# Hybrid decoder trunk: the first head pair's forget-gate projection ahead of its recurrence-gate products

## The chip, the cores and the metric

One Trainium2 chip, and one of its eight cores. The metric is the device time of one execution in microseconds (us); less is better. Five engines run side by side, each through its own instruction list in order: PE (matrix products), ACT (activations and copies), DVE (elementwise work on vectors), POOL (a second, slower elementwise engine), and SP, which here only issues transfers. They wait for each other through semaphores.

## The reference, cut to what matters

One layer on 1024 positions of width 1024: a norm, two token mixers side by side, a projection, then an MLP. The change touches the two mixers of one head pair:

```
proj = h @ w_in
xa, ga, q, f, v, g, m_a, m_b = jnp.split(proj, SPLIT_POINTS, axis=-1)
xa = causal_depthwise_conv(xa, conv_w, conv_b)
# first mixer: recurrence with two gates, one 256x256 block for each pair of heads
r = sigmoid(xb @ w_r + b_r);  i = sigmoid(xb @ w_i + b_i)
a = exp(-8 * r * softplus(-lam));  u = sqrt(-expm1(2 * log_a)) * (i * xf);  h = scan(a, u)
# second mixer: linear attention with a forget gate
f_gate = lb + (1 - lb) * sigmoid(f);  kf = (1 - lb) * sigmoid(-f);  qf = silu(q)
o = hgrn2_chunkwise(qf, kf, log(f_gate), v)
```

## The kernel before, in words

The mixers run in eight stages: two halves of the sequence (512 positions each, `c`) times four head pairs (256 channels, `p`); `stage(i)` with `i = 4c + p` issues the projections of one pair. A projection (`project_steps`) of a pair makes two PSUM banks of 128x512 from 16 pairs of 128x128 weights and 128x512 activations. Each product is done as three (high x high, high x low, low x high), for accuracy, so a projection is 48 products in eight pieces of six; between pieces the generator yields. The weights come in 128x1024 tiles: one transfer by SP, a cast on ACT (L94, the high part `wH`), and a subtraction on DVE (L98, the low part `wL`). Three such pairs of tiles fit at a time, so a cast waits for the products that read the tiles three earlier.

Stage 0 issues, in the order of the code: xa, the convolution of xa (`conv`, DVE L586, L98 for its split into `xcH` and `xcL`), q, five of the eight pieces of f, the products of the recurrence's gates (`rg_lru`: 24 products from `xcH`, `xcL` into `pr`, `pi` for each half `s` of the pair, four sigmoids, exp and tanh at L612, then DVE L633 to L644), the other three pieces of f, and `f_of` (two sigmoids of each bank at L671 and L672, which make `f` and `kk`, and DVE L673 and L674). Stage 0 runs alone.

Then `hgrn(i)` runs for each pair. It is mainly a chain on DVE (L681: products of decays with q and with k, into `qa`, `qb`, `kb`, `kc`, `kk`, `qf`), with a few blocks of small products on PE: three of scores (L691), then L811 and L822, transposes (L848), state updates (L858), outputs (L883, L886). `go(n)` issues n pieces of the next stage's projections ahead of such a block, so that PE has work while the chain goes on; for the first pair the numbers are GO_FIRST = (16, 5, 2, 1, 2), 16 pieces (xa and q of pair 1) to the third block and 5 more to L811. PE's order is held as the code has it, from the end of xa of stage 0 on. The orders of ACT and DVE are set by a scheduler when the program is built, from its own estimate of when each operand is ready, with the weight splits (`split_w`) at a higher priority.

PSUM banks come in rings by tag: `pj` has four (a projection takes two, and `pr`, `pi` of half 0 take two), `sc` two (`pr`, `pi` of half 1, and score blocks) and `hg` two.

Of the kernel before, what the change touches and what calls it, by code (L numbers as in the profile page):

```python
# [45 lines left out]
def trunk(ctx: ExitStack, tc: tile.TileContext, x, wts, mlp, pv, gains, mask_f, mask_u, out):  # L46
# [148 lines left out]
    def transposed(xn, dst, tt, name):  # L195
        for h in range(2):
            pt = bank("hg", f"xT_{name}_{h}")
            for k in range(4):
                pin(PE.transpose(pt[:, k * P : (k + 1) * P], xn[:, (4 * h + k) * P : (4 * h + k + 1) * P], ident))
            cut = slice(tt * P, (tt + 1) * P)  # L200
            split(pt.rearrange("p (k t) -> p k t", k=4), dst[0][h][:, :, cut], dst[1][h][:, :, cut])
# [59 lines left out]
    def parameters():  # L261

        tc.keep_in_program_order(V.tensor_tensor(out=t3, in0=lbl, in1=lbl, op=ALU.max))
        V.tensor_tensor(out=t3, in0=lbl, in1=t3, op=ALU.subtract)
        A.activation(t4, t3, AF.Sigmoid, scale=-1.0)
        A.activation(t3, t3, AF.Sigmoid)
        V.reciprocal(t4, t4)
        V.tensor_tensor(out=t3, in0=t3, in1=t4, op=ALU.mult)
        V.reciprocal(t4, t3)
        V.tensor_tensor(out=t3, in0=t3, in1=t4, op=ALU.mult)  # L270
        V.tensor_tensor(out=lb, in0=t3, in1=t3, op=ALU.subtract)
        V.tensor_scalar(lb, lb, 0.0, 1.0, op0=ALU.max, op1=ALU.min)
        V.tensor_scalar(omlb, lb, -1.0, 1.0, op0=ALU.mult, op1=ALU.add)

        V.tensor_scalar(t3, lam, -1.0, None, op0=ALU.mult)
        V.tensor_tensor(out=t4, in0=t3, in1=lam, op=ALU.min)
        A.activation(t4, t4, AF.Sigmoid)
        V.tensor_scalar(t5, t4, -1.0, 2.0, op0=ALU.mult, op1=ALU.add)
        V.reciprocal(t5, t5)
        V.tensor_tensor(out=t4, in0=t4, in1=t5, op=ALU.mult)  # L280
        V.tensor_tensor(out=t5, in0=t4, in1=t4, op=ALU.mult)
        V.tensor_scalar(t6, t5, 1.0 / 17, 1.0 / 15, op0=ALU.mult, op1=ALU.add)
        for n in (13, 11, 9, 7, 5, 3, 1):
            V.tensor_tensor(out=t6, in0=t6, in1=t5, op=ALU.mult)
            V.tensor_scalar(t6, t6, 1.0 / n, None, op0=ALU.add)
        V.tensor_tensor(out=t6, in0=t6, in1=t4, op=ALU.mult)
        V.tensor_scalar(t3, t3, 0.0, None, op0=ALU.max)
        V.scalar_tensor_tensor(t3, t6, 2.0, t3, op0=ALU.mult, op1=ALU.add)
        V.tensor_scalar(sp4, t3, 4.0, None, op0=ALU.mult)
        V.tensor_scalar(nsp8, t3, -8.0, None, op0=ALU.mult)  # L290
# [180 lines left out]
    def next_rows(tt, behind, square_behind=None):  # L471
        xt = tile_x(f"x{4 + tt}")
        nc.sync.dma_start(xt, x[(4 + tt) * P : (5 + tt) * P, :])
        xn = xt_pool.tile([P, D], F32, tag="xn", name=f"xn1{tt}", bufs=2)
        norm_rows(xt, xn, gain0[0], f"x1{tt}", behind, square_behind)
        return xn
# [30 lines left out]
    def combos_on(n):  # L507
        for _ in range(n):
            next(piece_parts.pop(0))

    def project_steps(c, name):

        pp = [bank("pj", f"pj_{name}_{s}") for s in range(2)]
        for half in range(2):
            wh, wl = next_w()
            for k in range(4):
                hh, hl = kt(hT[c], 4 * half + k)
                for s in range(2):
                    cols = slice(k * 256 + s * P, k * 256 + (s + 1) * P)
                    mm3(pp[s], wh[:, cols], wl[:, cols], hh, hl, half == 0 and k == 0, half == 1 and k == 3)  # L520
                if half == 0 or k < 3:
                    yield
        return pp
# [39 lines left out]
    def conv_in(c, p, pp):  # L563
        xc = mt("xc", f"xc{c}{p}", (P, 2, T))
        xps = []
        for s in range(2):
            u = 2 * p + s
            xp = mt("xp", f"xp{c}{u}", (P, T + 16), bufs=2)
            A.copy(xp[:, 3 : T + 3], pp[s])
            A.activation(  # L570
                xc[:, s, :],
                pp[s],
                AF.Identity,
                bias=pvt[:, PV_CB + u : PV_CB + u + 1],
                scale=pvt[:, PV_CW + 24 + u : PV_CW + 25 + u],
            )
            xps.append(xp)
        return xc, xps

    def conv(c, p, xc, xps, behind=None):  # L580
        for s in range(2):
            u = 2 * p + s
            xp = xps[s]
            V.tensor_copy(xp[:, 0:3], xcar[:, u, :])
            for j in range(3):
                ins = V.scalar_tensor_tensor(  # L586
                    xc[:, s, :],
                    xp[:, j : j + T],
                    pvt[:, PV_CW + 8 * j + u : PV_CW + 8 * j + u + 1],
                    xc[:, s, :],  # L590
                    op0=ALU.mult,
                    op1=ALU.add,
                )
                if behind is not None:
                    how = mybir.DependencyInfo(mybir.DependencyClass.NoSync, mybir.DependencyReason.DATA)
                    tc.add_manual_dep(ins.ins, behind.ins.name, how, reason="behind")
            if c + 1 < NC:
                G.tensor_copy(xcar[:, u, :], xp[:, T : T + 3])
        xh = mt("xcH", f"xcH{c}{p}", (P, 2, T), F32R)
        xl = mt("xcL", f"xcL{c}{p}", (P, 2, T), F32R)  # L600
        split(xc, xh, xl)
        return xc, xh, xl
# [311 lines left out]
    def hooked(steps, hooks):  # L914
        n = 0
        while True:
            try:
                next(steps)
            except StopIteration as end:
                return end.value  # L920
            n += 1
            if n in hooks:
                hooks[n]()
            yield

    def v_of(i):
        def between(tt):
            if tt == 0:
                gots[i - 1]["tail"]()
            if tt == (2 if i == 2 else 1):  # L930
                on_T(*where(i - 2), gots[i - 2])
            for n in {}.get((i, tt), ()):
                with tc.high_priority(400):
                    transposed(xn1[n], hT[1], n, f"x1{n}")

        yield from v_steps(*where(i - 1), gots[i - 1], between)

    def stage(i):
        c, p = where(i)
        got = gots[i]  # L940
        if i > 1:
            yield from v_of(i)

        def more(n):
            with tc.high_priority(400):
                transposed(xn1[n], hT[1], n, f"x1{n}")

        hooks = {at: lambda n=n: more(n) for at, n in {2: ((4, 1),), 3: ((2, 2), (6, 3))}.get(i, ())}
        px = yield from hooked(project_steps(c, f"xa{c}{p}"), hooks)
        xc, xps = conv_in(c, p, px)  # L950
        if i == 0:
            parameters()
            tc.keep_in_program_order(V.tensor_copy(mu, mu32.to_broadcast([P, 7, 8, 32])))
            pinned[0] = True
        yield
        if i == 1:
            gots[0]["tail"]()
            transposed(xn1[0], hT[1], 0, "x10")
        if i > 4:
            combos_on(2)  # L960

        def convolve():
            got["xc"] = conv(c, p, xc, xps, None)

        pq = yield from hooked(project_steps(c, f"q{c}{p}"), {} if i == 1 else {6: convolve})
        got["q1"] = q_of(c, p, pq)
        yield
        fs = hooked(project_steps(c, f"f{c}{p}"), {6: convolve} if i == 1 else {})
        for _ in range(5 if i != 1 else 7):
            next(fs)  # L970
            yield
        if i > 3:
            combos_on(1 if i == 4 else 2)
        if i == 1:
            pf = yield from fs
            got["f"], got["kk"] = f_of(c, p, pf)
            yield
        yield from rg_lru(c, p, got, *got["xc"])
        if i > 0:
            gots[i - 1]["normalised"]()  # L980
        for n in ((0,), (1,), (2, 3))[i] if i < 3 else ():
            if i == 0:
                xn1[n] = next_rows(n, behind_first[1], behind_first[0])
            else:
                xn1[n] = next_rows(n, gots[0]["states"] if i == 1 else None)
        if i != 1:
            pf = yield from fs
            got["f"], got["kk"] = f_of(c, p, pf)

# [770 lines left out]
    for kb in range(n_kb):  # L1760
        last = kb + 1 == n_kb
        qs = order[2 * kb : 2 * kb + 2]
        for half in range(2):
# [33 lines left out]
            for step, (bk, wo, uo), prs in [  # L1797
# [14 lines left out]
                for pr in prs:  # L1812
                    _, ci, cj, op = ADDS[step]
# [95 lines left out]
```

## Time and profile before

| what | value |
|---|---|
| time, median of 3 runs | 1535.8 us (1534.24 to 1536.2) |
| the profiled execution's own time | 1535.65 us |
| its span on the profile | 1533.9 us |
| granted clock of PE in it | 0.999 |
| busy in the span: PE, DVE, ACT, POOL | 99%, 75%, 53%, 10% |

The profile is of one execution. A page gives busy times, the chain of work that ended last and the costliest groups; a trace behind it lists every instruction with its start and, in brackets, how long its engine had stood still before it and what ended that. Names are those of the program without numbers, so `pj_f` is either bank of the projection f, of whichever stage runs then. Stage 0 takes the first 64 us or so, pair 0's `hgrn` goes on to about 113 us. Starts of consecutive products lie closer than their lengths, since PE overlaps them.

### The profile page before, as it was taken

What the parts mean: (1) busy time and instruction counts of PE and PEld (TensorE: products, weight loads), DVE (VectorE), ACT (ScalarE), POOL (GpSimd) and SP (SyncE); (2) the same over time, 40 slices, a digit from 0 to 9 for tenths busy, and PEclk for the clock granted to TensorE, in tenths of its full rate; (3) what the DMA queues carried; (4) which work ended last, traced back from release to release, by engine and by line L of the source; (5) the groups of instructions that cost most, each with busy time, mean ns of one, the idle gap of its engine ahead of it and who ended that gap; (6) DMA issues with size and microseconds to landing.
All of it is one profiled execution on the core that took longest, in us unless ns stands there. A gap on an engine that the chain in (4) does not pass through costs nothing. (4 is left out here: it accounts for less than half of the span.)

```text
span 1533.9 us, 23245 instructions
## 1 busy us (share of the span) xinstructions
PE 1521.5 (99%) x9091; PEld 1275.1 (83%) x9091; DVE 1148.0 (75%) x1661; ACT 806.4 (53%) x1346; POOL 152.3 (10%) x191
## 2 busy tenths in 40 slices
PE   9999999999999999999999999999999999999998
PEld 7878988889889888888888888888888888888886
DVE  6798696485675828786856568888788998888777
ACT  6646757567567435454533447766666722111115
POOL 1021210232614600000000000000000000000000
PEclk9999999999999999999999999999999999999999
DMA  8545455465664284432328323666666766666642
GB/s 300 198 154 200 143 193 198 150 217 173 226 230 143 97 299 160 159 137 83 138 97 327 138 110 145 267 247 247 247 252 249 262 259 264 252 248 249 240 194 110
DMA packets 82255, 306.82 MB, mean 200 GB/s; under 512 B 8545, under 2 KB 21985, under 8 KB 69218
## 3 DMA queue, kind: packets, MB, share of 16 engines
q1 hardware_dynamic: 78832, 295.24, 52.2%
q10 hardware_dynamic: 3314, 10.10, 1.7%
q8 instruction: 71, 1.16, 0.3%
q14 instruction: 38, 0.31, 0.1%
HBM read 201.50 MB, written 103.81 MB: 199 GB/s over the span
## 5 line engine op out<-in xcount | busy, mean ns | idle before, releaser
L1795 DVE TENSOR_TENSOR acc<-acc,dX 128x512 f32<-128x512 f32 x128 | 85.1, 685 | 27.7 <-PE dX L157 27.0
L94 ACT CAST wA<-q 128x512 fp32r<-128x512 f32 x46 | 28.6, 622 | 119.3 <-PE dX L157 95.4
L98 DVE TENSOR_TENSOR wL<-raw,wH 128x1024 fp32r<-128x1024 f32 x46 | 56.2, 1224 | 41.1 <-ACT wH L94 40.9
L157 PE MATMUL po<-wH,y 128*128 128x512 f32 x256 | 80.6, 391 | 0.0
L94 ACT CAST wH<-raw 128x1024 fp32r<-128x1024 f32 x46 | 48.2, 1049 | 34.2 <-DMA raw<-wts_in 14.2
L1695 POOL TENSOR_TENSOR gx<-acc,gain 128x256 f32<-128x256 f32 x1 | 0.7, 743 | 605.4 <-DVE acc L1795 605.4
L157 PEld LDWEIGHTS po<-wH,y 128*128 128x128 f32 x256 | 48.1, 188 | 9.8
L1795 DVE TENSOR_TENSOR acc<-acc,dY 128x512 f32<-128x512 f32 x64 | 43.6, 687 | 14.2 <-PE dY L157 13.8
L157 PE MATMUL po<-wL,y 128*128 128x512 f32 x128 | 49.8, 389 | 0.0
L1543 ACT ACTIVATE b<-b 128x512 f32<-128x512 f32 x48 | 30.0, 626 | 28.3 <-DVE b L1542 28.1
L98 DVE TENSOR_TENSOR wA<-q,wA 128x512 fp32r<-128x512 f32 x46 | 31.5, 686 | 15.1 <-ACT wA L94 15.1
L157 PE MATMUL uX<-h2B11H,wA 128*128 128x512 f32 x128 | 42.1, 390 | 0.0
L120 ACT CAST wH<-raw 128x1024 fp32r<-128x1024 f32 x36 | 37.8, 1049 | 8.2 <-issue 3.7
L192 POOL TENSOR_TENSOR rstd_h<-rstd_h,mhalf 128x1 f32<-128x1 f32 x8 | 4.6, 585 | 371.2 <-DVE rstd_h L187 371.2
L586 DVE SCALAR_TENSOR_TENSOR xc<-xp,pvt,xc 128x512 f32<-128x512 f32 x48 | 40.0, 844 | 1.1 <-ACT xc L570 1.1
L157 PE MATMUL gX<-hT00H,wA 128*128 128x512 f32 x112 | 36.9, 390 | 0.0
L1102 DVE TENSOR_TENSOR s<-q,q 128x512 f32<-128x512 f32 x46 | 31.6, 687 | 5.1 <-DMA q<-mlp_in 4.8
L499 POOL TENSOR_TENSOR stt<-r,stt 128x256 fp32r<-128x256 f32 x16 | 19.8, 1261 | 126.3 <-ACT stt L498 114.2
L1110 DVE TENSOR_TENSOR s<-q 128x512 f32<-128x512 f32 x46 | 31.6, 686 | 0.2
L1544 ACT ACTIVATE b<-b 128x512 f32<-128x512 f32 x48 | 30.3, 631 | 1.0
L890 ACT ACTIVATE on<-po 128x128 f32<-128x128 f32 x64 | 16.9, 278 | 26.1 <-PE po L886 26.0
L157 PEld LDWEIGHTS uX<-h2B11H,wA 128*128 128x128 f32 x128 | 24.0, 188 | 5.0
(2327 smaller groups left out, 5298.8 us busy)
## 6 DMA issues: line engine op xcount, KB each, us to landing
q<-mlp_in SPq DMA_DIRECT2D x92, 512.0 KB, 3.8
raw<-wts_in SPq DMA_DIRECT2D x80, 512.0 KB, 4.7
rest<-wL SPq DMA_DIRECT2D x36, 512.0 KB, 2.9
wL<-rest SPq DMA_DIRECT2D x36, 512.0 KB, 4.0
hd<-ri SPq DMA_DIRECT2D x16, 256.0 KB, 3.7
od<-onT ACTq DMA_DIRECT2D x8, 512.0 KB, 6.5
cdT<-stT SPq DMA_DIRECT2D x16, 256.0 KB, 3.4
o<-od SPq DMA_DIRECT2D x4, 1024.0 KB, 7.8
```

The lines of the kernel that those rows point to most:

```text
L94: ins = casts[name] = A.copy(h, src)
L98: ins = V.tensor_tensor(out=lo, in0=src, in1=h.bitcast(F32), op=ALU.subtract)
L120: A.copy(h, raw)
L157: ins = PE.matmul(o, a, b, start=begins, stop=ends, **how)
L499: G.tensor_tensor(out=lo, in0=src, in1=h.bitcast(F32), op=ALU.subtract)
L586: ins = V.scalar_tensor_tensor(xc[:, s, :], xp[:, j : j + T], pvt[:, PV_CW + 8 * j + u : PV_CW + 8 * j + u + 1], xc[:, s, :], op0=ALU.mult ...
L890: A.activation(on[:, 4 * s + n, :], po[s][:, n * P : (n + 1) * P], AF.Square, accum_out=ssq[:, 4 * s + n : 4 * s + n + 1],)
L1102: ins = V.tensor_tensor(out=sa[:, 0, :], in0=a21, in1=a22, op=ALU.add)
L1110: V.tensor_tensor(out=sb[:, 0, :], in0=a21, in1=a11, op=ALU.add)
L1543: A.activation(b[:, at, :], b[:, at, :], AF.Relu, scale=-1.0 if at == 2 else 1.0)
L1544: A.activation(b[:, at, :], b[:, at, :], AF.Square)
L1795: return V.tensor_tensor(out=dst, in0=dst, in1=banks[bk, pr], op=op)
```

## The change

Stage 0 now does what stage 1 already did: all eight pieces of f and `f_of` are issued before `rg_lru`. No other stage is changed, and no instruction of the projections is added or left out.

```
-        for _ in range(5 if i != 1 else 7):
+        for _ in range(5 if i > 1 else 7):
             next(fs)
             yield
         if i > 3:
             combos_on(1 if i == 4 else 2)
-        if i == 1:
+        if i < 2:
             pf = yield from fs
             got["f"], got["kk"] = f_of(c, p, pf)
             yield
...
-        if i != 1:
+        if i > 1:
             pf = yield from fs
             got["f"], got["kk"] = f_of(c, p, pf)
```

On PE 24 gate products and the last 18 products of f change places. On ACT and DVE the scheduler rearranges pair 0's work up to about 105 us of the trace; behind that all lists are as before.

The first place is on ACT, where f's products end (`f_649`, `kk_650` are pair 0's f and kk; `rw`, `ri` its two gates; `wH_660` the cast of pair 1's second xa tile):

```order
 L94 CAST wH_619<-raw_617 128x1024
-L612 ACTIVATE rw_639<-pr_643,pvt 128x512
-L612 ACTIVATE ri_640<-pi_644,pvt 128x512
-L612 ACTIVATE rw_639<-pr_659,pvt 128x512
-L94 CAST wH_633<-raw_631 128x1024
-L612 ACTIVATE ri_640<-pi_660,pvt 128x512
+L671 ACTIVATE f_649<-pj_f_0_583 128x512
+L94 CAST wH_660<-raw_658 128x1024
+L672 ACTIVATE kk_650<-pj_f_0_583 128x512
+L671 ACTIVATE f_649<-pj_f_1_584 128x512
+L672 ACTIVATE kk_650<-pj_f_1_584 128x512
+L612 ACTIVATE rw_666<-pr_670,pvt 128x512
```

The sigmoids of f stood behind exp, tanh and a table load for them; now they are ahead of the gates' sigmoids, and one ACT_TABLE_LOAD (at L671) is gone.

The second place is on DVE a little before L822's operand `qf` is made. These are the convolution's products of pair 1's second half (`xc_811<-xp_815`), level masks of pair 0 (`dd_718`) and `kc_735`:

```order
 L584 COPY xp_815<-xcar 128x3
 L584 COPY xp_1576<-xcar 128x3
+L586 SCALAR_TENSOR_TENSOR xc_811<-xp_815,pvt,xc_811 128x512
+L710 COPY_PREDICATED dd_718<-mu,sc_00_928 128x32x6
+L586 SCALAR_TENSOR_TENSOR xc_811<-xp_815,pvt,xc_811 128x512
+L710 COPY_PREDICATED dd_718<-mu,sc_00_928 128x32x4
+L586 SCALAR_TENSOR_TENSOR xc_811<-xp_815,pvt,xc_811 128x512
+L710 COPY_PREDICATED dd_718<-mu,sc_00_928 128x32x2
 L681 TENSOR_TENSOR kc_735<-kc_735,seg_720 128x32x24
```

Three convolution products of pair 1, which came behind `qf`, now come ahead of `kc` and so of `qf`.

The third place is ACT between the last `qf` copy and the sigmoids of pair 1 (`kT` are the transposed keys that L858 reads):

```order
+L94 CAST xcH_1137<-xc_811 128x1024
 L790 COPY qf_1023<-qb_727 128x16x32
 L94 CAST wH_1074<-raw_1072 128x1024
 L827 COPY scT<-sc_00_1086 32x8x32 x2
 L828 COPY scT<-sc_00_1103 64x8x64
-L94 CAST xcH_1137<-xc_811 128x1024
 L853 COPY kT_1157<-pk_1147 128x512
 L853 COPY kT_1157<-pk_1148 128x512
```

The cast of pair 1's convolution stood ahead of the `kT` copies and now stands ahead of the `qf` copy.

More of the change, by code (lines that the diff above doesn't have):

```diff
@@ L968, in stage @@
         fs = hooked(project_steps(c, f"f{c}{p}"), {6: convolve} if i == 1 else {})
-        for _ in range(5 if i != 1 else 7):
+        for _ in range(5 if i > 1 else 7):
             next(fs)
@@ L973, in stage @@
             combos_on(1 if i == 4 else 2)
-        if i == 1:
+        if i < 2:
             pf = yield from fs
@@ L985, in stage @@
                 xn1[n] = next_rows(n, gots[0]["states"] if i == 1 else None)
-        if i != 1:
+        if i > 1:
             pf = yield from fs
```

## The prediction

> **What bounds the kernel now.** I read the page first, then busy time by stages, then what PE waited for, then the timeline of PE at each of those waits, and last DVE and ACT around them.
>
> ```profile
> PE 1521.5 (99%) x9091; PEld 1275.1 (83%) x9091; DVE 1148.0 (75%) x1661; ACT 806.4 (53%) x1346; POOL 152.3 (10%) x191
> ...
> 80.00:100.00 20.00, 19.41 (x305) 15.35 (x304) 20.00 (x42) 7.92 (x12) 2.74 (x3) 1.00 0.42 154
> 100.00:120.00 20.00, 18.88 (x125) 16.61 (x124) 17.55 (x35) 13.69 (x34) 8.74 (x8) 1.00 0.39 132
> 120.00:140.00 20.00, 20.00 (x188) 17.86 (x187) 18.21 (x30) 14.02 (x29) 1.79 (x3) 1.00 0.60 214
> ...
> PE po L883 <- DVE sn L869: 0.9, 1, 0.9
> PE dX L157 <- DMA u8n<-u8n: 0.7, 1, 0.7
> PE sc L822 <- DVE qf L681: 0.5, 1, 0.5
> ...
> PE pkv L858 <- ACT kT L853: 0.2, 1, 0.2
> ```
>
> The first line is the page's busy time: PE works 1521.5 of 1533.9 us. The next three are stretches of 20 us (length, then PE, PEld, DVE and ACT busy, then POOL, the granted clock, DMA): PE is full from 120 us on, and between 80 and 120 us it stands for 0.59 + 1.12 = 1.7 us, with DVE full at first. The last four are waits of PE over the whole run (total, times, longest); the only longer one is at the start. Three of these, 0.9, 0.5 and 0.2 us, lie in pair 0's `hgrn` and wait for DVE or ACT. So the kernel is bound by PE; what this change can win is time in which PE waits for pair 0's chain, and what it can lose is a new wait on PE. All later work is PE at full, so a shift at 113 us should reach the end.
>
> The waits in brackets leave out part of the loss. Pair 1 runs the same blocks without a wait, so the two can be laid side by side:
>
> ```profile
> 95.97 0.39 PE L157 MATMUL pj_f<-hT01H,wL 128*128 128x512 f32 x1
> ...
> 97.64 1.12 PE L822 MATMUL sc<-qf,kk 128*64 128x64 f32 x16 [0.51 <-DVE qf L681]
> 98.69 0.50 PE L157 MATMUL pj_f<-hT01H,wH 128*128 128x512 f32 x1
> ...
> 103.61 0.39 PE L157 MATMUL pj_f<-hT01H,wL 128*128 128x512 f32 x1
> ...
> 105.98 0.48 PE L157 MATMUL pr<-xcH,wH 128*128 128x512 f32 x1
> ...
> 108.61 0.39 PE L157 MATMUL pi<-xcH,wL 128*128 128x512 f32 x1
> 109.93 0.68 PE L883 MATMUL po<-v,scT 128*128 128x128 f32 x4 [0.93 <-DVE sn L869]
> ...
> 113.05 0.47 PE L157 MATMUL pr<-xcH,wH 128*128 128x512 f32 x1
> ...
> 152.49 0.39 PE L157 MATMUL pj_q<-hT01H,wL 128*128 128x512 f32 x1
> ...
> 153.43 1.15 PE L822 MATMUL sc<-qf,kk 128*64 128x64 f32 x16
> 154.51 0.50 PE L157 MATMUL pj_q<-hT01H,wH 128*128 128x512 f32 x1
> ...
> 160.75 0.39 PE L157 MATMUL pj_f<-hT00H,wL 128*128 128x512 f32 x1
> ...
> 162.68 0.48 PE L157 MATMUL pj_f<-hT00H,wH 128*128 128x512 f32 x1
> ...
> 163.91 0.40 PE L157 MATMUL pj_f<-hT00H,wL 128*128 128x512 f32 x1
> ...
> 167.18 0.48 PE L157 MATMUL pj_f<-hT01H,wH 128*128 128x512 f32 x1
> ```
>
> From the last projection product ahead of a block to the first behind it, pair 0 takes 98.69 - 95.97 = 2.72 us at L811 and L822, 105.98 - 103.61 = 2.37 at L858, and 113.05 - 108.61 = 4.44 at L883. Pair 1 takes 2.02, 1.93 and 3.27. The losses are **0.70, 0.44 and 1.17 us, 2.31 together**. That is the most that a faster chain of pair 0 can give, 0.15% of the time.
>
> **The change part by part.**
>
> *PE.* It removes and adds nothing; 18 products of f pass ahead of 24 gate products.
>
> ```profile
> 59.30 0.39 PE L157 MATMUL pi<-xcH,wL 128*128 128x512 f32 x1
> ...
> 63.38 0.39 PE L157 MATMUL pj_f<-hT01H,wL 128*128 128x512 f32 x1
> ```
>
> From the last gate product to the last of f's are 18 products in 63.38 - 59.30 = 4.08 us, 0.227 each; the 24 gate products take 5.44. So f's last product starts at 57.94 in place of 63.38, 5.44 us earlier, and the last gate product 4.08 later, at 63.38. Their sum is the same, and PE does not wait between them in the trace. The gates' operand `xcL` is subtracted by DVE long before. Cost: nothing, if the banks hold (rival 3). The moved pieces issue no weight transfer: f's second tile is asked for in its fifth piece, which stays, and so SP's list keeps its order but for one: both transfers of the scanned `ri` now stand ahead of one store of a `wL`, and nothing on PE reads either in this stretch. POOL's list is unchanged.
>
> *ACT and DVE, up to `qf`.* Both lists start f's work earlier and end the gates' work later.
>
> ```profile
> 60.59 1.23 DVE L98 TENSOR_TENSOR wL<-raw,wH 128x1024 fp32r<-128x1024 f32 x1 [5.53 <-ACT wH L94]
> ...
> 64.76 1.23 DVE L98 TENSOR_TENSOR wL<-raw,wH 128x1024 fp32r<-128x1024 f32 x1 [1.81 <-ACT wH L94]
> ...
> 67.91 0.55 DVE L673 TENSOR_SCALAR f<-f,par 128x512 f32<-128x512 f32 x1
> ...
> 70.28 0.88 DVE L681 TENSOR_TENSOR q<-q,f 128x512 f32<-128x512 f32 x1
> ...
> 80.21 0.74 DVE L681 TENSOR_TENSOR qb<-qa,seg 128x256 f32<-128x256 f32 x2
> ...
> 96.82 0.67 DVE L681 TENSOR_TENSOR qf<-qb,seg 128x512 f32<-128x512 f32 x1
> ...
> 97.69 0.73 DVE L586 SCALAR_TENSOR_TENSOR xc<-xp,pvt,xc 128x512 f32<-128x512 f32 x1
> ```
>
> These are DVE's rows, with its two idle times in brackets; ACT's are:
>
> ```profile
> 60.45 0.68 ACT L612 ACTIVATE ri<-pi,pvt 128x512 f32<-128x512 f32 x1
> 61.15 1.28 ACT L612 ACT_TABLE_LOAD   x1
> ...
> 64.63 1.33 ACT L612 ACTIVATE rw<-rw,par 128x512 f32<-128x512 f32 x2
> 65.98 1.28 ACT L671 ACT_TABLE_LOAD   x1
> 67.27 0.60 ACT L671 ACTIVATE f<-pj_f 128x512 f32<-128x512 f32 x1
> ```
>
> The first sigmoid of f ran at 67.27, 3.5 us after f's end, behind exp, tanh and a table load. After the change f's first bank is complete near 57.7, and its sigmoid of 0.60 is done at about 58.2; DVE can begin f there. Between 58.2 and the end of `qf` (97.49) DVE stood still for 2.4 us (the part of the 5.53 behind 58.2) and for 1.81; the other 35.1 us were work. All of that work is still ahead of `qf`, and three convolution products of 0.73 (2.2 us) are new ahead of it. Gaps that I expect: 0.7 us, since the second weight split waits for its cast, which stands behind the first sigmoid. So `qf` ends near 58.2 + 35.1 + 2.2 + 0.7 = 96.2, which is **1.3 us earlier**.
>
> PE wants it at 95.97 + (153.43 - 152.49) = 96.9. So the 0.70 us at L822 go, with 0.7 us to spare. The bounds of this term are the full 0.70 and, if DVE's 4.2 us of idle all came back in other places, qf at 58.2 + 35.1 + 2.2 + 4.2 = 99.7, which is 2.2 us later than now (rival 2). I take the first, because of where DVE could wait: at its first operation on tanh's result. In the trace the chain from q's product to the `qb` products fills 70.28 to 80.95, 10.7 us, with two weight splits, one gate operation and `kc` in between. The new list has the same there, one gate operation and two splits included, but `kc` (about 1 us) behind and f's three (about 0.6 each) ahead. That is about 11.5 us, and with the gap of 0.7 DVE comes to tanh's result near 58.2 + 12.2 = 70.4. Tanh ends at 63.38 + 0.39 (the last gate product) + 1.05 (a weight cast listed there) + 0.68 (`ri`) + 1.28 (table) + 2 x 1.33 (exp and tanh) = 69.4, 1.0 us ahead.
>
> [...]
>
> *Behind `qf`: L858 and L883.*
>
> ```profile
> 102.59 1.05 ACT L94 CAST xcH<-xc 128x1024 fp32r<-128x1024 f32 x1 [3.22 <-DVE xc L586]
> ...
> 104.50 0.61 ACT L671 ACTIVATE f<-pj_f 128x512 f32<-128x512 f32 x1
> ...
> 107.68 0.28 DVE L867 COPY sn<-pkv 128x128 f32<-128x128 f32 x1
> ```
>
> The cast at 102.59 held the two `kT` copies back, L858 waited for them, and pair 1's f sigmoid waited behind them until 104.50, though f's first bank was complete near 103.61 - 3 x 0.23 + 0.39 = 103.3. The cast now runs before `qf`'s copy, since the convolution is done by then. So the `kT` copies follow the transposes at once and the **0.44 us go**. The sigmoid moves to where its bank is complete, 103.3 - 0.7 = 102.6, so 1.8 to 1.9 us earlier, and behind it, by DVE's order, a weight split, f's second half and then `sn`, from 107.68 to about 105.85. The first output product came 109.93 - 107.68 = 2.25 us behind it, which gives 108.1. PE is ready for it at 108.61 + 0.23 - 0.70 - 0.44 = 107.7. So 0.4 us of the 1.17 stay and **0.77 go**. Bounds: 0 (the chain moves only as far as PE does) and 1.17.
>
> **Sum:** 0.70 + 0.44 + 0.77 = 1.9 us. Against the profiled execution, 1535.65 - 1.9 = 1533.75, say **1533.8 us**. The median of the runs shown is 1535.80, 0.15 above that execution, which is less than the spread of the runs, 1.96.
>
> **The rivals.**
>
> 1. *PE gets its time back and hands it to a later wait, or the chain ends no earlier.* For it: DVE is full from 80 to 100 us, so work moved ahead of `qf` is work PE waits for. Against it: no wait on PE from 120 to 140 us, nor a later one longer than 0.7. The time stays at 1535.65.
>
> 2. *Slower: DVE waits for tanh.* The gates' sigmoids, exp and tanh end 3.4 us later than now (69.4 against 64.63 + 1.33 = 66.0), and their DVE work stands ahead of `qf`, as do the three convolution products. From 0.7 us of such standing on, L822 waits again; from 1.3 on it waits longer than now. At the bound, `qf` at 99.7, PE loses 2.2 us more: 1537.9. Against it: DVE has pair 0's own chain to do before that operation.
>
> 3. *PSUM banks.* f holds two of four `pj` banks, and pair 1's xa wants two at 63.6. Before, xa could take two banks that the gates' first sigmoids had read out ahead of the `ri` at 60.45; now ACT must read f's or those out first. f's are read by about 60.8 (four sigmoids and a cast of 1.05 from 57.7), so 2.8 us are spare. If xa had to wait for the last sigmoid, `ri` at 65.3, PE would stand 1.7 us: 1533.75 + 1.7 = 1535.5. [...]
>
> 4. *That it does not do what it says* is ruled out by the lists: f and `hgrn`'s first products are ahead of the gates' work on both engines.
>
> **How the numbers follow.** The forecast, a gain of 1.2 to 2.31 us, gets 0.65; rival 1 0.17, rival 2 0.09, rival 3 0.05, and 0.04 is left for what I do not see. Its own range is 1533.3 to 1534.5. The range that is to hold 8 in 10 goes from 1532.3, the cap of 2.31 less about 1 us, half the spread of the runs, to 1537.0, which takes in rivals 1 and 3 and half of rival 2. 0.2% is 3.07 us, about what a measurement can tell here: faster means below 1532.7, which the cap of 2.31 does not reach without luck in the runs, 0.07; slower means above 1538.9, beyond rival 2's bound, 0.03; within it, 0.90.
>
> **What would show it.** Right: pair 0's three stretches on PE (2.72, 2.37, 4.44) at 2.0, 1.9 and 3.7; f's first sigmoid near 57.7; `qf` done near 96.2 with no wait at L822; two table loads between 50 and 75 us where there were three. Wrong: a wait on PE at the start of pair 1's xa (rival 3), DVE idle for ACT around 70 us and `qf` behind 97 (rival 2), or the three stretches shorter and the span not, with a new wait behind 113 us (rival 1).

## The result, and the profile after

The changed kernel takes 1543.88 us (median of 5 runs, 1543.21 to 1545.23), the kernel before 1535.2 us in the same session (5 runs, 1534.24 to 1536.2). The ratio is 1.0058, with an interval of 1.0046 to 1.0069: it is **slower by 8.7 us**, where 1.9 us faster was forecast. The profiled execution of the changed kernel took 1545.23 us, the slowest of its five.

The page's first lines and the list of PE's waits (total, times, longest) of the changed kernel:

```profile
span 1543.5 us, 23241 instructions
PE 1524.7 (99%) x9091; PEld 1276.1 (83%) x9091; DVE 1148.6 (74%) x1661; ACT 805.0 (52%) x1345; POOL 156.7 (10%) x191
```
```profile
PE gY L157 <- DMA gt1H<-cdt: 4.2, 1, 4.2
...
PE gY L157 <- DMA gt1L<-cdt: 1.7, 1, 1.7
PE gX L157 <- DMA gT4L<-cdT: 1.6, 1, 1.6
PE xT_x L364 <- DVE xn L355: 0.7, 1, 0.7
PE gX L157 <- DMA gn2L<-cdn: 0.3, 1, 0.3
PE po L883 <- DVE sn L869: 0.3, 1, 0.3
```

PE waits on four transfers that were not in the list before, 4.2 + 1.7 + 1.6 + 0.3 = 7.8 us, and all of them stand in a stage that the change does not touch. Of the three waits in pair 0's `hgrn`, those at L822 and L858 are gone and the one at L883 has gone from 0.9 to 0.3.

So the profile has two stories. The first is where the prediction looked. Pair 0's three stretches on PE in the changed kernel (start, length, engine, line, operation, tiles):

```profile
96.35 0.39 PE L157 MATMUL pj_f<-hT01H,wL 128*128 128x512 f32 x1
...
97.30 1.15 PE L822 MATMUL sc<-qf,kk 128*64 128x64 f32 x16
98.38 0.50 PE L157 MATMUL pj_f<-hT01H,wH 128*128 128x512 f32 x1
...
103.25 0.39 PE L157 MATMUL pj_f<-hT01H,wL 128*128 128x512 f32 x1
103.48 1.95 PE L858 MATMUL pkv<-v,kT 128*128 128x128 f32 x16
105.18 0.48 PE L157 MATMUL pr<-xcH,wH 128*128 128x512 f32 x1
...
107.77 0.39 PE L157 MATMUL pi<-xcH,wL 128*128 128x512 f32 x1
108.44 0.68 PE L883 MATMUL po<-v,scT 128*128 128x128 f32 x4 [0.28 <-DVE sn L869]
...
111.55 0.48 PE L157 MATMUL pr<-xcH,wH 128*128 128x512 f32 x1
```

The stretches are now 98.38 - 96.35 = 2.03 us, 105.18 - 103.25 = 1.93 and 111.55 - 107.77 = 3.78, where they were 2.72, 2.37 and 4.44. That is 1.79 us won, of the 1.9 forecast.

The second story is at 555 us, where the two mixers end and the products of the gate of the MLP begin. Its operands are combinations of quarter matrices which POOL makes and which are stored to memory as `cdt`, `cdn` and `cdT`; SP loads them, in one fixed order, into new tiles: `gt1H`, `gt1L`, `gn2H`, `gn2L`, `gT3H`, `gT3L`, `gT4H`, `gT4L` (`load_combo`, first for `t1`, `n2` and `T3`, later for `T4`). First these loads on SP, of the kernel before, then of the changed one:

```profile
535.96 0.33 SPq L1156 DMA_DIRECT2D gt1H<-cdt  x1
539.45 0.33 SPq L1156 DMA_DIRECT2D gt1L<-cdt  x1
```
```profile
555.29 0.33 SPq L1156 DMA_DIRECT2D gt1H<-cdt  x1
555.67 0.53 SPq L1156 DMA_DIRECT2D gt1L<-cdt  x1
...
564.90 0.33 SPq L1156 DMA_DIRECT2D gT4L<-cdT  x1
```

The first load leaves 19.3 us later. SP's rows keep their order in both traces, so the seven other loads of these tiles leave later too: `gT3L` at 558.66 in place of 548.66, `gT4L` at 564.90 in place of 561.62. What SP waited for is in SP's own list of waits from 530 to 570 us, of the kernel before (one row) and of the changed one (one row):

```profile
SPq L1156 <- DVE sn L869: 10.7, 1, 10.7
```
```profile
SPq L1156 <- DVE g L1026: 29.9, 1, 29.9
```

L1026 is the last gate of the mixers, `g = g * smb`, whose operand is the sigmoid `smb` made at L1025. The row of DVE in the changed kernel, and PE's rows where the load is wanted:

```profile
554.00 1.22 DVE L1026 TENSOR_TENSOR g<-g,smb 128x1024 f32<-128x1024 f32 x1
```
```profile
557.82 0.39 PE L157 MATMUL gZ<-hT01H,wA1234L 128*128 128x512 f32 x1
562.44 0.80 PE L157 MATMUL gY<-gt1H,ws134H 128*128 128x512 f32 x1 [4.24 <-DMA gt1H<-cdt]
564.93 0.79 PE L157 MATMUL gY<-gt1L,ws134H 128*128 128x512 f32 x1 [1.69 <-DMA gt1L<-cdt]
565.52 0.63 PE L157 MATMUL gY<-gt1H,ws134L 128*128 128x512 f32 x1
565.95 0.63 PE L157 MATMUL gY<-gt1H,ws134H 128*128 128x512 f32 x1
...
569.12 0.39 PE L157 MATMUL gX<-gn2H,ws134H 128*128 128x512 f32 x1
```

L1026 ends at 554.00 + 1.22 = 555.22, and `gt1H` is issued at 555.29. PE would have come to it at 557.82 + 0.23 = 558.05; it starts at 562.44.

Why a load of `gt1H` waits for a reader of `smb` stands in no list of instructions. It is a matter of places in SBUF. Tiles of the mixers come from one pool, by tag; a tag gets its place when its first tile is made, and `smb` is made with the tag of the gates' `ri` (`t = mt("ri", f"smb{c}", (P, 2, T))`). The change makes `kk` (in `f_of`) ahead of the tiles of `rg_lru`, so three tags change places. The built programs give these addresses, in bytes of each partition; `gt1H` belongs to a later pool that lies over the same space:

```
                  before                 after
190208 to 194304  ri, and smb            kk
194304 to 198400  rr, and kT             ri, and smb
198400 to 202496  kk                     rr, and kT
196352 to 204544  gt1H, later            gt1H, later
```

Before, `ri` and its late tenant `smb` lay below `gt1H`. Now the upper half of `ri` lies under it, so the load waits for the last reader of `smb`, which is the 29.9 us of SP's row. All other tiles of this pool lie where they lay. The weights' tiles, which belong to another pool, exchange places among themselves as well; the first experiment below keeps that and loses nothing by it.

The stretches of busy time show what follows (length, then PE, PEld, DVE, ACT, POOL, the granted clock, the DMA share, GB/s), of the kernel before and of the changed one:

```profile
540.00:555.00 15.00, 15.00 (x72) 12.51 (x71) 4.20 (x5) 8.13 (x22) 1.65 (x1) 1.00 0.96 357
```
```profile
540.00:555.00 15.00, 15.00 (x72) 12.52 (x71) 5.20 (x5) 8.18 (x17) 1.43 (x1) 1.00 0.09 36
555.00:560.00 5.00, 3.21 (x15) 2.32 (x13) 0.22 (x1) 0.59 (x1) 0.00 (x0) 1.00 0.95 302
560.00:565.00 5.00, 0.86 (x2) 0.36 (x2) 0.69 (x1) 0.00 (x0) 0.00 (x0) 0.65 1.01 425
565.00:570.00 5.00, 4.71 (x13) 3.48 (x14) 0.00 (x0) 0.58 (x1) 0.00 (x0) 0.67 1.02 431
```

From 540 to 555 us the transfers used to run at 357 GB/s; now they stand nearly still, at 36. Afterwards all loads are asked for within 10 us and the transfer engines are full, at 425 and 431 GB/s with shares of 1.01 and 1.02. One load of 1024 KB takes 1.05 MB / 425 GB/s = 2.5 us at that rate, which is just the time from the first product on `gt1H` to the first on `gt1L`, 564.93 - 562.44 = 2.49.

The whole loss can be counted between two points of PE: the last product ahead of the first one on `gt1H`, and the first product of the next group of weights on it (`ws135`). The rows of the tile `gt1H` for that group in the kernel before and the changed one give its first and last start:

```profile
L157 PE MATMUL gY<-gt1H,ws135H x4: 389/389/389, 575.5 to 577.6; 128*128 128x512 f32 x4
```
```profile
L157 PE MATMUL gY<-gt1H,ws135H x4: 389/389/389, 585.6 to 587.7; 128*128 128x512 f32 x4
```

With the row of before that stands ahead of it,

```profile
558.99 0.39 PE L157 MATMUL gZ<-hT01H,wA1234L 128*128 128x512 f32 x1
```

the same work took 575.5 - 558.99 = 16.5 us before and takes 585.6 - 557.82 = 27.8 now: **11.3 us lost**, while PE came there 558.99 - 557.82 = 1.17 us earlier. The 11.3 are 4.4 us until the first product, 4.0 more in the twelve products with `gt1` (6.68 us from 562.44 to 569.12, where twelve at 0.227 make 2.72), and 2.9 behind them, of which 0.3 + 1.6 are the waits for `gn2L` and `gT4L`. Of the 4.0, 2.3 are the late `gt1L`, whose first product starts 2.49 us behind the one before it in place of 0.227. The other 1.7 are products at a granted clock of 0.50 (the mean of every stretch from 562 to 568 us), 565.95 - 565.52 = 0.43 us apart: the eleven from 564.93 to 569.12 take 4.19 us in place of 2.50.

Less the 1.17 us this leaves PE 10.1 us late. At the group of weights after that (`ws136`, first product at 595.1 before and 604.7 now) it is 9.6 us late, and so is the end: the spans are 1533.9 and 1543.5 us.

### The profile page after: what moved, and what is told of

Same layout as the page of the kernel before. It is cut to its first block, busy times and chain, and to the rows that moved or that the text cites. A ratio compares the mean times of both kernels' runs of the same rounds, so it can differ in the third digit from the quotient of the medians.

```text
span 1543.5 us, 23241 instructions
## 1 busy us (share of the span) xinstructions
PE 1524.7 (99%) x9091; PEld 1276.1 (83%) x9091; DVE 1148.6 (74%) x1661; ACT 805.0 (52%) x1345; POOL 156.7 (10%) x191
## 5 line engine op out<-in xcount | busy, mean ns | idle before, releaser
L1192 DVE TENSOR_TENSOR gb<-gY,ge 128x512 f32<-128x512 f32 x14 | 9.7, 691 | 30.7 <-PE gY L157 30.7
```

## The experiments

The theory was that the place of `ri` alone makes the loss. Its rivals: that the new order of ACT and DVE makes it, that another of the moved tags does, or that PE comes earlier to a load that cannot come earlier. The first five kernels keep every engine's order as in the changed kernel or in the one before, and differ in places only; the sixth moves one load, and behind it a few casts and sums of the gate stage change places on ACT and DVE.

### The changed kernel with the old places

The four tags of `rg_lru` get their places first, as before; the order of the work is that of the change.

```
# in stage(i), ahead of f's last piece
+        if i == 0:
+            got["places"] = {t: mt(t, f"{t}{c}{p}", (P, 2, T)) for t in ('rw', 'ri', 'rr', 'h')}
# in rg_lru
-        w, ig, e = (mt(t, f"{t}{nm}", (P, 2, T)) for t in ("rw", "ri", "rr"))
-        a = mt("h", f"a{nm}", (P, 2, T))
+        places = got["places"] if "places" in got else {}
+        w, ig, e, a = (places[t] if t in places else mt(t, f"{t}{nm}", (P, 2, T)) for t in ("rw", "ri", "rr", "h"))
```

> The changed kernel, with the four tiles of the recurrence's gates (rw, ri, rr, h) reserved in stage 0 ahead of kk, as the kernel before does. Every engine's list is that of the changed kernel; only the places of kk, ri and rr in SBUF go back. Theory PLACE (the load gt1H lies over the place of ri and so waits for its last tenant, smb of the last stage): gt1H issued near 535, no wait on PE at gt1H, pair 0's gain of 1.5 to 1.9 us stays, 1533.3 to 1533.8 us. Rival TIME (the load is late because the change moves the transfers or DVE's work in time): as the changed kernel, 1543 to 1545 us.

Measured: 1533.5 us (11 runs, 1532.6 to 1534.41) against 1535.11 for the kernel before (21 runs), ratio 0.9988 (0.998 to 0.9997). The first load, and the two longest of PE's waits over the whole run:

```profile
534.53 0.33 SPq L1158 DMA_DIRECT2D gt1H<-cdt  x1
```
```profile
PE gain L331 <- POOL gain_row L321: 2.5, 1, 2.5
PE xT_x L364 <- DVE xn L355: 0.4, 1, 0.4
```

The load leaves at 534.53 and no load of the gate stage holds PE; of the waits that are left the two longest stand at the start, and the one at L883 is 0.3 us. The same order of work with the old places is **faster than before by 1.8 us** by the ratio (0.5 to 3.1; the medians lie 1.6 us apart), which is what the three stretches give. So the order of ACT and DVE costs nothing later.

### The kernel before with the new places

This is the other half: the order of before, with only `kk` reserved first.

```
# in stage(i), ahead of rg_lru
+        if i == 0:
+            got["kk_place"] = mt("kk", f"kk{c}{p}", (P, 2 * T))
# in f_of
-        kk = mt("kk", f"kk{c}{p}", (P, 2 * T))
+        kk = gots[4 * c + p].get("kk_place") or mt("kk", f"kk{c}{p}", (P, 2 * T))
```

> The kernel before, with kk's tile of stage 0 reserved ahead of rw, ri and rr and nothing else: every engine's list is that of the kernel before. PLACE: gt1H issued behind the last product with smb, near 556, PE waits 4 us and more for it, 10 to 11 us slower than before, 1545 to 1546.5 us. TIME: as before, 1535.2 us.

Measured: 1545.88 us (4 runs, 1545.78 to 1546.37), ratio 1.0068 (1.0054 to 1.0082). `gt1H` is issued at 557.38. From PE's waits:

```profile
PE gY L157 <- DMA gt1H<-cdt: 4.2, 1, 4.2
...
PE gY L157 <- DMA gt1L<-cdt: 1.7, 1, 1.7
PE po L883 <- DVE sn L869: 0.9, 1, 0.9
...
PE sc L822 <- DVE qf L681: 0.5, 1, 0.5
```

No instruction has moved, and the loss is whole: 10.8 us over before. It carries the waits at L822 and L883 of before and the new ones as well. So the loss does not need PE to come earlier.

### The changed kernel with `smb` in another place

`smb` moves to the tag `q1`, below all that `gt1H` covers; nothing else moves.

```
-            t = mt("ri", f"smb{c}", (P, 2, T))
+            t = mt("q1", f"smb{c}", (P, 1536))[:, 0 : 2 * T].rearrange("p (a b) -> p a b", a=2)
```

> The changed kernel with its places as they are, but smb (the sigmoid of the last gate) put into the place of q1 in place of that of ri. PLACE, with smb as the one tenant that holds the load: gt1H issued near 535, 1533.3 to 1533.8 us. If another tenant of kk's, ri's or rr's places holds it as well: gt1H between 540 and 555 and some of the 8 us stays. TIME: 1543 to 1545 us.

Measured: 1533.69 us (10 runs, 1532.84 to 1534.69), ratio 0.9989 (0.998 to 0.9998). SP's row says when the load left:

```profile
534.60 0.33 SPq L1156 DMA_DIRECT2D gt1H<-cdt  x1
```

PE waits for no load of the gate stage. So `smb` is the one tenant of `ri` that matters; the places of `kk`, `rr` and `kT` are as in the changed kernel here and cost nothing.

### `ri` wholly under the load

The order of places is `kk`, `rr`, `ri`, by reserving `rw`, `rr` and `ri` in this order ahead of `rg_lru`; `ri` then lies at 198400 to 202496, wholly under `gt1H`.

```
# in stage(i), ahead of rg_lru (rg_lru as in the first experiment)
+        if i == 0:
+            got["places"] = {t: mt(t, f"{t}{c}{p}", (P, 2, T)) for t in ("rw", "rr", "ri")}
```

> The changed kernel with the three places in the order kk, rr, ri: ri then lies wholly under gt1H (in the changed kernel half of it does), rr half. PLACE: the load waits for smb all the same, 1543 to 1545 us. If it is kk's being first, or how far ri lies under the load, that counts: other than that by several us. TIME: 1543 to 1545 us as well, so this run tells PLACE from the old order alone together with the first.

Measured: 1543.74 us (4 runs, 1543.56 to 1544.19), ratio 1.0054 (1.0038 to 1.0069). `gt1H` is issued at 555.00 and PE waits 3.9 us for it. Half of `ri` under the load (the changed kernel, 1543.88 us) or all of it (1543.74) is the same here, since L1026 reads all of `smb` in one instruction, late.

### `ri` first, `kk` second

Only `rw` and `ri` are reserved ahead of f's last piece, so `ri` has its old place and `kk` and `rr` have changed theirs against before.

```
# in stage(i), ahead of f's last piece (rg_lru as in the first experiment)
+        if i == 0:
+            got["places"] = {t: mt(t, f"{t}{c}{p}", (P, 2, T)) for t in ('rw', 'ri')}
```

> The changed kernel with the three places in the order ri, kk, rr: neither the old order (ri, rr, kk) nor the new one (kk, ri, rr), but ri at its old address, clear of gt1H. PLACE (only where ri lies counts): gt1H issued near 535, no wait at gt1H, 1533.3 to 1534.0 us. If the old order itself is needed, as where kk's or rr's last reader also holds the load: gt1H later than 540 and some of the 8 us stays.

Measured: 1532.96 us (10 runs, 1532.26 to 1533.42) against 1534.91 (14 runs), ratio 0.9987 (0.9977 to 0.9997). `gt1H` leaves at 534.68 and no load holds PE. This median is the lowest of all versions, but its interval lies over that of the first experiment, so the two are alike. The place of `ri` is all there is to it.

### The held load last

In the changed kernel, with its places, `gt1H` is asked for behind `gt1L`, `gn2` and `T3`. If most of the loss comes from the loads that queue behind it on SP (the head of the line), it should nearly go; if it is the load's own wait, it should stay.

```
-                for o in ("t1", "n2", "T3"):
+                in_turn(gop["t1"][1].bitcast(F32), cd["t1"][:, 1])
+                for o in ("n2", "T3"):
                     load_combo(o)
+                in_turn(gop["t1"][0].bitcast(F32), cd["t1"][:, 0])
```

> The changed kernel with its places, but the held load gt1H issued behind gt1L, gn2H, gn2L, gT3H and gT3L in SP's list and not ahead of them. Theory HEAD OF THE LINE (most of the loss is that seven more loads stand behind the held one and then go out together at the full rate): the other five go out from 538 to 548, gt1H alone at 555.3, lands 3 to 5 us later with nothing beside it, PE waits 0.3 to 2.5 us, its clock is not lowered; 1534 to 1536.5 us. Rival OWN WAIT (the loss is the held load's own lateness): gt1H lands near 562 as in the changed kernel, PE waits over 4 us; 1541 us and more.

Measured: 1541.04 us (5 runs, 1539.09 to 1543.08), ratio 1.0041 (1.0028 to 1.0054). The five other loads leave from 537.71 to 546.00; `gt1H` does not, and of the loads PE waits for it alone. SP's row, then PE's:

```profile
554.62 0.32 SPq L1156 DMA_DIRECT2D gt1H<-cdt  x1
```
```profile
563.29 0.79 PE L157 MATMUL gY<-gt1H,ws134H 128*128 128x512 f32 x1 [5.71 <-DMA gt1H<-cdt]
...
568.23 0.39 PE L157 MATMUL gX<-gn2H,ws134H 128*128 128x512 f32 x1
```

So queueing behind the held load makes some 1543.88 - 1541.04 = 2.8 us of the loss, and the load's own wait with the lower clock behind it (0.50 granted from 562 to 564 us) makes the rest. The 2.8 is rough, since the runs of this kernel lie up to 4.0 us apart and its interval overlaps that of the changed kernel. The expectation that the loss nearly goes failed, and its rival came (a wait of over 4 us, 1541 us and more). It turns on one number. Had the load landed as it did before, 5.1 us behind its issue, PE would have waited until 559.7 in place of 563.29; it took 8.6 us. Two stores of the mixers' last results and weights of the MLP moved beside it. One of the stores is that of `g` to `g2d`: `g` is the result of the same L1026, so the store left at 554.62 with the load, and landed 8.8 us later. How much of the 8.6 us comes from this company was not tried and stays open.

## Why the prediction was wrong, and where it was right

**The terms were right.** Each can be read off the changed kernel:

| step | predicted | measured |
|---|---|---|
| f's first sigmoid starts | 57.7 | 58.07 |
| tanh ends; DVE comes to its result | 69.4; 70.4 | 69.50; 70.28, no wait |
| `qf` ends | 96.2 | 96.17, no wait at L822 |
| the stretch at L811 and L822 | 2.0 | 2.03 |
| the stretch at L858 | 1.9 | 1.93 |
| the stretch at L883 | 3.7 | 3.78 |
| table loads between 50 and 75 us | 2 | 2 |

```profile
58.07 0.60 ACT L671 ACTIVATE f<-pj_f 128x512 f32<-128x512 f32 x1 [3.89 <-PE pj_f L157]
...
68.18 1.32 ACT L612 ACTIVATE rw<-rw,par 128x512 f32<-128x512 f32 x2
```
```profile
70.28 0.68 DVE L634 TENSOR_SCALAR rw<-rw 128x1024 f32<-128x1024 f32 x1
...
95.49 0.68 DVE L681 TENSOR_TENSOR qf<-qb,seg 128x512 f32<-128x512 f32 x1
```

These are ACT's and DVE's rows of the changed kernel. The sigmoid is 0.37 us late because PE started later here: its wait for the first operand, `xT_x`, was 0.7 us in this execution and 0.2 in that of before. That `qf` still ends within 0.03 us of the forecast is partly luck: DVE began f 0.5 us later than forecast (58.71 for 58.2), stood still for 0.4 us in place of 0.7 and worked 0.2 us less. Rivals 2 and 3 did not come: DVE came 0.8 us behind tanh, and PE waits for no bank between 58 and 70 us. Rival 4 did not come either.

**The step that failed** is the one from pair 0 to the end: "All later work is PE at full, so a shift at 113 us should reach the end." The shift did reach 555 us (PE came there 1.17 us earlier), and there the changed kernel waits for a load that the trace of before shows as hidden, and takes 11.3 us longer for the same work. I had taken the change to be its order of instructions. The order behind 105 us is indeed as before; what the instructions wait for is not, because `f_of` ahead of `rg_lru` also changes which tag gets its place first. With that one effect undone the forecast holds: the first experiment gains 1.8 us (1533.5 us), where 1.9 were forecast (1533.8 us).

Rival 1 had the right sign to look for, "the three stretches shorter and the span not, with a new wait behind 113 us", but for another reason. It let PE give back at most what it had won, at 1535.65 us; the second experiment shows the loss with nothing won, 10.8 us. The 0.04 kept for the unseen was too small, and the range, made of the sizes of known terms, had no room for an effect of another kind: its upper end is 6.9 us under the result. The price could have been read beforehand. This is DVE's row in the trace of before:

```profile
555.16 1.22 DVE L1026 TENSOR_TENSOR g<-g,smb 128x1024 f32<-128x1024 f32 x1
```

There `gt1H` is issued at 535.96, lands 5.1 us later and is wanted at 559.2, one product behind the 558.99, so it had some 18 us to spare. Behind L1026, which ends at 556.38, it lands at 561.5 if it again takes 5.1 us, so PE would stand for 2.3 us or more. To ask this of L1026 at all, the addresses of both programs have to be compared.

## What to carry to other kernels

An edit that makes a tile earlier in the code may move its pool's places, and with them the waits of loads that come much later and into another pool over the same space: beside the order, compare the addresses, and what each later load waits for. Where an order of places works, reserve it on its own lines, so that the order of the work can change without it. A tag that serves several uses holds its place until the last of them, and a load laid over it waits for that one, as `gt1H` did here: issued at 555.29 in place of 535.96.

## What the runs showed of the hardware

Where PE waits for `gt1H` in these runs, the wait costs more than its length, since PE comes back at a granted clock of 0.50. In the sixth experiment PE stands still from 563.29 - 5.71 = 557.58 us; the stretches of 2 us show the granted clock (third number from the end):

```profile
558.00:560.00 2.00, 0.00 (x0) 0.00 (x0) 0.00 (x0) 0.00 (x0) 0.00 (x0) 1.00 0.95 379
560.00:562.00 2.00, 0.00 (x0) 0.00 (x0) 0.00 (x0) 0.00 (x0) 0.00 (x0) 0.74 0.98 406
562.00:564.00 2.00, 0.70 (x2) 0.61 (x3) 0.41 (x1) 0.00 (x0) 0.00 (x0) 0.50 0.25 100
```

If the clock fell in one step from 1.00 to 0.50, the mean of 0.74 puts the step near 561.0, 3.4 us after PE stopped. The twelve products behind it then took 568.23 - 563.29 = 4.94 us in place of 2.72, so 2.2 us were lost to the clock although no load was missing any more. The time from the stop to the step is not the same in every run. Reckoned in the same way, it is 3.3 us in the changed kernel (PE stands from 558.20, and the mean is 0.87 from 560 to 562), but less in the second and the fourth experiment, one row each:

```profile
562.00:564.00 2.00, 0.00 (x0) 0.00 (x0) 0.00 (x0) 0.00 (x0) 0.00 (x0) 0.68 1.02 428
```
```profile
560.00:562.00 2.00, 0.22 (x1) 0.22 (x1) 0.64 (x1) 0.00 (x0) 0.00 (x0) 0.63 1.02 430
```

In the second PE stands from 564.50 - 4.21 = 560.29 us, and 0.68 puts the step near 562.7, 2.4 us later; in the fourth it stands from 561.78 - 3.88 = 557.90, and 0.63 gives 560.5, 2.6 us later. So here the clock was already lowered after 2.4 us of standing in one run, and only after 3.4 in another. The low clock then lasted 6.8 us in the sixth experiment (to 567.8, as the mean of 0.72 from 565 to 570 says) and 10.2 us in the second (to 572.9, with 0.71 from 570 to 575). No run here shows what sets these times. PE's waits in the kernel before, in pair 0's chain, were all under 1 us (0.9, 0.5 and 0.2), and the clock stayed at 1.00 there, from 80 to 120 us.
